# Products with the values in a hybrid attention encoder: the two heads of a pair alternate on TensorE, and the sample's third key tile has 128 rows

## The chip, the cores and the metric

One core of one Trainium2 chip runs the kernel. The metric is the device time of one execution in microseconds (us). One core has TensorE (matrix products), VectorE, ScalarE and GpSimd (elementwise work), SyncE, which mostly issues DMAs, and 16 DMA engines.

## The reference

One step of a two-layer encoder for two request groups that share the weights: a prompt of 256 frames and a sample of 32 frames with 256 cached ones behind it. The model width is 1024, the heads have 64 features, everything is float32.

- Even layer: one input projection feeds 8 heads of chunk-band attention (A) and 8 heads of forgetting attention (B), both with a softmax; then an output projection.
- Odd layer: 16 heads of stick-breaking attention (C): weights from a sum of log-sigmoids over the keys between, no softmax.
- After each: cross-attention into 256 memory tokens (4 heads of 256 features) and a squared-ReLU MLP of width 4096, all with RMS norms and residual adds.

The change concerns the last step of A, B and C, the weighted sum of values:

```python
p = jax.nn.softmax(s, axis=-1).astype(v.dtype)          # A and B
return jnp.einsum('bhqk,bkhd->bqhd', p, v)
...
w = jnp.where(before, jnp.exp(jax.nn.log_sigmoid(z) + tail), 0.0)   # C
return jnp.einsum('bhqk,bkhd->bqhd', w.astype(v.dtype), v)
```

## The kernel before

Activations lie transposed, features on partitions, 288 columns: 256 frames of the prompt and 32 of the sample. Each projection is computed in chunks of 256 output features. A chunk of weights (two tiles "raw") is loaded by SyncE's queue and split into a high part wh (fp32r, ScalarE or VectorE, L143 and L145) and a low part wl (VectorE or GpSimd, L146). A projection is then three products per 128 x 128 block, L160 to L162, into a PSUM tile "g" of 288 columns (256 for the memory's keys and values).

An attention group has four heads, in two pairs p; the two heads of a pair (par = 0, 1) lie in the two halves of 128 partitions. The even layer has groups A0, A1, B0, B1 (`attend_ab`), the odd layer four groups C (`attend_c`). What follows is done per group:

- Scores. In A and B, "ss" holds the sample's scores (L501 and L502: heads of pair 0 into partitions 0 to 63, pair 1 into 64 to 127), and "s" the prompt's scores of one head (L524, L525). In C, "za" and "zb" hold a pair's prompt scores, keys on partitions, and "zs" the sample's (L626, L629 and then L636 to L640).
- Softmax of A and B on VectorE and ScalarE into "pr" (prompt, one head) and "prs" (sample, four heads), then three transposes on TensorE (L530 to L532, L538 to L540) and a copy by ScalarE to "pt" and "pts" in SBUF. In C the weights "w" and "ws" come out with keys on partitions: an ACTIVATE (Exp) and an AFFINE_SELECT on GpSimd that zeroes the upper triangle (L566).
- Products with the values. The stationary operand is a 128 x 64 block of values (one key tile, one head), the moving one the weights. `pv_prompt` is called once per head and issues the product of the first key tile with 256 queries (L469) and of the second with 128 (L470). `pv_sample` issues, for each of four heads, a product with two cached key tiles of 128 rows (L478, L479) and one with the sample's own 32 keys (L480), each with 32 columns. The results stand in the half of the PSUM tile ("po", "za", "pos", "zs") that belongs to the head: partitions 0 to 63 or 64 to 127.
- Evacuation by ScalarE (high part "oh") and VectorE (low part "ol"), which the output projection reads.

The values of the frames are computed by `project_v` into "vT" and transposed into "vt", three key tiles of 256 features; of the third only rows 0 to 31 are written. The cached values "cv" come by DMA.

The program's order on each engine is made by a scheduler when the kernel is built, from the code's order, the pools' buffer counts and its own estimates of time; the two strings ORD_AB and ORD_C give the order in which projections ("q", "p"), groups ("a") and keys of the memory ("K") are handed to it. On an engine, instructions run in that order. "pr" has PRB = 4 buffers, "pt" PTB = 2, "vt" VTB = 2.

## Time and profile before

| | |
|---|---|
| median of 3 runs | 983.2 us (981.46 to 984.86) |
| profiled execution | 983.06 us, span 981.4 us |
| TensorE busy | 971.2 us (99%), 7276 matmul records |
| VectorE busy | 680.5 us (69%) |
| ScalarE busy | 541.6 us (55%) |
| GpSimd busy | 247.7 us (25%) |
| DMA | 160.03 MB, 163 GB/s on average |

The span is the time from the first to the last instruction of the profiled execution; the rest of its 983.06 us lies around it. PE is TensorE's matmuls, PEld its weight loads, DVE VectorE, ACT ScalarE, POOL GpSimd, SP SyncE. A form such as 128*64 behind an operation of PE says how many rows and columns of the array the instruction uses; what follows is the moving operand's size. L12 is line 12 of the kernel.

### The profile page before, as it was taken

Reading aid. Unit: us, or ns where it says so; the run is one execution under the profiler, and the core shown is the slowest. Engines: PE = TensorE matmul, PEld = TensorE weight load, DVE = VectorE, ACT = ScalarE, POOL = GpSimd, SP = SyncE. Lnnn points to the kernel's source line nnn. Section 1 sums busy time; section 2 is a strip of 40 time slices with the busy share of each in tenths; the row PEclk is TensorE's granted clock in tenths of the full one; section 3 lists DMA queues with packets and bytes.
Section 4 is the critical chain, followed back from the end, with each engine's and each line's share of the span. In section 5 each row is a group of like instructions: output and inputs, shape, how many; then the busy total and the mean of one; then the engine's idle time right before and its main releaser. Section 6 shows DMA issues by size and latency. Waiting matters only on the chain.

```text
span 981.4 us, 19371 instructions
## 1 busy us (share of the span) xinstructions
PE 971.2 (99%) x7276; PEld 935.6 (95%) x7276; DVE 680.5 (69%) x1460; ACT 541.6 (55%) x1272; POOL 247.7 (25%) x275
## 2 busy tenths in 40 slices
PE   8999999999999999999999999999999999999998
PEld 8998888899999999999999888889999999999998
DVE  7778778679587767676786555758996766564643
ACT  5667666556456635454656567746554665453531
POOL 4321562222112221122122332323443211111110
PEclk9999999999999999999999999999999999999999
DMA  8654454654545545545565434246444555545552
GB/s 265 198 177 148 146 165 161 213 163 144 172 160 170 169 158 169 168 156 170 170 213 170 144 121 142 97 154 207 145 147 135 169 164 163 166 161 171 168 170 74
DMA packets 50702, 160.03 MB, mean 163 GB/s; under 512 B 6296, under 2 KB 12968, under 8 KB 50352
## 3 DMA queue, kind: packets, MB, share of 16 engines
q1 hardware_dynamic: 46864, 148.69, 47.3%
q0 software_dynamic: 2592, 8.92, 2.4%
q10 hardware_dynamic: 1152, 1.18, 0.4%
q8 instruction: 57, 0.93, 0.4%
q14 instruction: 37, 0.30, 0.1%
HBM read 148.65 MB, written 10.12 MB: 162 GB/s over the span
## 4 chain that ended last, share of the span: by engine, by line
PE 97%; DVE 1%; DMA 1%; ACT 0%; issue 0%; SPq 0%; ACTq 0%; DVEq 0%
PE g L160 28%; PE g L162 27%; PE g L161 27%; PE po L469 1%; PE za L469 1%; PE s L524 1%; PE za L586 1%; DMA raw<-in_w_kv_dram 1%; PE zs L626 0%; PE sx L160 0%; PE za L607 0%; PE sx L162 0%; DMA raw<-in_ab_w_dram 0%; PE pox L162 0%; PE ps_px L698 0%; PE pos L478 0%
## 5 line engine op out<-in xcount | busy, mean ns | idle before, releaser
L145 ACT ACTIVATE wh<-raw 128x512 fp32r<-128x512 f32 (+3 forms) x561 | 279.5, 550 | 231.7 <-PE g L161 120.8
L146 DVE TENSOR_TENSOR wl<-raw,wh 128x512 fp32r<-128x512 f32 (+3 forms) x483 | 306.6, 669 | 111.9 <-ACT wh L145 106.2
L146 POOL TENSOR_TENSOR wl<-raw,wh 128x512 fp32r<-128x512 f32 (+2 forms) x141 | 177.0, 1255 | 540.7 <-ACT wh L145 438.3
L161 PE MATMUL g<-xl,wh 128*128 128x288 f32 (+1 forms) x1032 | 304.0, 297 | 1.5 <-DVE xl L198 1.5
L160 PE MATMUL g<-xh,wh 128*128 128x288 f32 (+1 forms) x1032 | 302.8, 298 | 0.7 <-DVE vT L429 0.4
L162 PE MATMUL g<-xh,wl 128*128 128x288 f32 (+1 forms) x1032 | 302.0, 297 | 0.0
L161 PEld LDWEIGHTS g<-xl,wh 128*128 128x128 f32 (+1 forms) x1032 | 193.6, 188 | 2.6 <-DVE xl L198 1.8
L160 PEld LDWEIGHTS g<-xh,wh 128*128 128x128 f32 (+1 forms) x1032 | 192.6, 188 | 2.4 <-DVE vT L429 0.7
L162 PEld LDWEIGHTS g<-xh,wl 128*128 128x128 f32 (+1 forms) x1032 | 192.9, 188 | 1.1 <-issue 0.2
L161 PE MATMUL g<-hl,wh 128*128 128x288 f32 x512 | 150.3, 295 | 0.0
L160 PE MATMUL g<-hh,wh 128*128 128x288 f32 x512 | 148.9, 295 | 0.0
L162 PE MATMUL g<-hh,wl 128*128 128x288 f32 x512 | 148.5, 294 | 0.0
L161 PEld LDWEIGHTS g<-hl,wh 128*128 128x128 f32 x512 | 96.1, 188 | 0.0
L162 PEld LDWEIGHTS g<-hh,wl 128*128 128x128 f32 x512 | 95.7, 188 | 0.0
L160 PEld LDWEIGHTS g<-hh,wh 128*128 128x128 f32 x512 | 95.3, 187 | 0.0
L161 PE MATMUL g<-ol,wh 128*128 128x288 f32 x256 | 75.7, 298 | 0.0
L160 PE MATMUL g<-oh,wh 128*128 128x288 f32 x256 | 74.6, 299 | 0.6 <-ACT oh L488 0.6
L162 PE MATMUL g<-oh,wl 128*128 128x288 f32 x256 | 74.6, 298 | 0.0
L781 DVE TENSOR_TENSOR h<-h,g 128x288 f32<-128x288 f32 x64 | 28.8, 450 | 29.6 <-PE g L162 29.5
L160 PEld LDWEIGHTS g<-oh,wh 128*128 128x128 f32 x256 | 48.0, 190 | 1.0 <-ACT oh L488 0.8
L162 PEld LDWEIGHTS g<-oh,wl 128*128 128x128 f32 x256 | 48.3, 191 | 0.6 <-issue 0.6
L161 PEld LDWEIGHTS g<-ol,wh 128*128 128x128 f32 x256 | 48.8, 190 | 0.0
(323 smaller groups left out, 1554.8 us busy)
## 6 DMA issues: line engine op xcount, KB each, us to landing
raw<-in_w_up_dram SPq DMA_DIRECT2D x64, 512.0 KB, 3.8
raw<-in_w_down_dram SPq DMA_DIRECT2D x64, 512.0 KB, 3.8
raw<-in_w_kv_dram SPq DMA_DIRECT2D x32, 512.0 KB, 3.9
raw<-in_sb_w_dram SPq DMA_DIRECT2D x24, 512.0 KB, 4.5
raw<-in_ab_w_dram SPq DMA_DIRECT2D x22, 512.0 KB, 4.8
raw<-in_w_q_dram SPq DMA_DIRECT2D x16, 512.0 KB, 4.5
raw<-in_w_o_dram SPq DMA_DIRECT2D x16, 512.0 KB, 4.0
raw<-in_ab_wo_dram SPq DMA_DIRECT2D x8, 512.0 KB, 3.9
```

Source lines behind the costliest of these rows:

```text
L145: act(wh[:, r, :], src, AF.Copy)
L146: e.tensor_tensor(wl[:, r, :], src, wh[:, r, :].bitcast(F32), ALU.subtract)
L160: mm(out, lh, rh, start=first, stop=False)
L161: mm(out, lh, rl, start=False, stop=False)
L162: return mm(out, ll, rh, start=False, stop=last)
L469: mm(dst[:, 0:NP_], vt[:, 0, cols], pt0, start=True, stop=False)
L524: mm(s[:, 0:NP_], q[:, P:NP_], kT[:, p, 0:NP_], start=True, stop=True)
L586: mm(za2, x[:, 0:P], y, start=f_, stop=False, skip_group_check=True)
L781: dve.tensor_tensor(h[:, kt, :], h[:, kt, :], ps[:, 0:T], ALU.add)
```

## The change

`pv_prompt` takes both heads of a pair at once and issues, for each key tile, first head 0 and then head 1. In A and B it is called after the second head's softmax and copy, so "pt" of both heads must be kept (PTB = 3). `pv_sample` goes over key tiles first, then pairs, then heads, and its third product has all 128 rows: the third tile of "vt" is zeroed by a memset before its 32 rows are written, "prs" becomes a tile of 384 columns in the ring of "pr" whose last 96 columns are zeroed, and in C the columns of "ws" that hold the third tile are zeroed. The third transpose of the sample's weights thereby has the full form, and one copy brings all three to SBUF. The branches under SR = 0, which are never taken, are removed.

```diff
-PTB = 2
+PTB = 3
...
         vt = R.ph.tile([P, 3, CW], F32, tag="vt", name="vt", bufs=VTB)
+
+        nc.gpsimd.memset(vt[:, 2, :], 0.0)
...
-    def pv_prompt(po, par, p, vt, pt0, pt1):
-
-        cols = slice(p * P + 64 * par, p * P + 64 * par + 64)
-        dst = po[64 * par:64 * par + 64, :]
-        mm(dst[:, 0:NP_], vt[:, 0, cols], pt0, start=True, stop=False)
-        mm(dst[:, P:NP_], vt[:, 1, cols], pt1, start=False, stop=True)
-
-    def pv_sample(po, cv, vt, pts, pcol):
-        for p in range(2):
+    def pv_prompt(po, p, vt, pts):
+        for kk in range(2):
             for par in range(2):
                 cols = slice(p * P + 64 * par, p * P + 64 * par + 64)
-                dst = po[64 * par:64 * par + 64, p * NS:(p + 1) * NS]
-                q = slice(pcol(p, par), pcol(p, par) + NS)
-                mm(dst, cv[:, 0, cols], pts[0][:, q], start=True, stop=False)
-                mm(dst, cv[:, 1, cols], pts[1][:, q], start=False, stop=False)
-                mm(dst, vt[0:NS, 2, cols], pts[2][0:NS, q], start=False, stop=True)
+                mm(po[64 * par:64 * par + 64, kk * P:NP_], vt[:, kk, cols], pts[par][kk], start=kk == 0, stop=kk == 1)
+
+    def pv_sample(po, cv, vt, pts, pcol):
+        vs = (cv[:, 0, :], cv[:, 1, :], vt[:, 2, :])
+        for kk in range(3):
+            for p in range(2):
+                for par in range(2):
+                    cols = slice(p * P + 64 * par, p * P + 64 * par + 64)
+                    q = slice(pcol(p, par), pcol(p, par) + NS)
+                    mm(po[64 * par:64 * par + 64, p * NS:(p + 1) * NS], vs[kk][:, cols], pts[kk][:, q],
+                       start=kk == 0 and p == 0, stop=kk == 2, skip_group_check=True)
...
-        prs = scr.tile([P, T], F32, tag="f", bufs=FB, name="prs")
-        softmax_rows([s[:, 0:T]], [bsmp], [prs], 1)
+        prs = R.ph.tile([P, 384], F32, tag="pr", name="prs", bufs=PRB)
+        nc.gpsimd.memset(prs[:, T:384], 0.0)
+        softmax_rows([s[:, 0:T]], [bsmp], [prs[:, 0:T]], 1)
         for p in range(2):
-            po = bank(R.o, "po")
+            pts = []
             for par in range(2):
...
-                pv_prompt(po, par, p, vt, pt[:, 0:NP_], pt[:, NP_:NP_ + P])
+                pts.append((pt[:, 0:NP_], pt[:, NP_:NP_ + P]))
+            po = bank(R.o, "po")
+            pv_prompt(po, p, vt, pts)
             put_prompt(oh, ol, kt0 + p, po)
...
-        nc.tensor.transpose(pp[0:NS, 2 * P:3 * P], prs[:, NP_:T], ident)
+        for kk in range(3):
+            nc.tensor.transpose(pp[:, kk * P:(kk + 1) * P], prs[:, kk * P:(kk + 1) * P], ident)
         pt = R.ph.tile([P, 384], F32, tag="pt", bufs=PTB, name="pts")
-        act(pt[:, 0:2 * P], pp[:, 0:2 * P], AF.Copy)
-        act(pt[0:NS, 2 * P:3 * P], pp[0:NS, 2 * P:3 * P], AF.Copy)
+        act(pt, pp[:, 0:3 * P], AF.Copy)
...
-            for par in range(2):
-                pv_prompt(po, par, p, vt, w[:, par * NP_:(par + 1) * NP_], w[:, 512 + par * P:512 + (par + 1) * P])
+            pv_prompt(po, p, vt, [(w[:, par * NP_:(par + 1) * NP_], w[:, 512 + par * P:512 + (par + 1) * P])
+                                  for par in range(2)])
...
         w = R.ph.tile([P, 768], F32, tag="pr", name="ws", bufs=4)
+        nc.gpsimd.memset(w[:, 2 * P:384], 0.0)
```

The order on TensorE changes in three ways. Line numbers of the changed kernel are others: its L473 is L469 and L470 of before, L483 is L478 to L480, L505 and L506 are L501 and L502, L516 and L517 are L524 and L525, L522 to L524 are L530 to L532, L159 to L161 are L160 to L162, L618 and L621 are L626 and L629, and L533 is L538 to L540.

The first place is the sample's products of the third group of the odd layer ("zs" is their PSUM tile, "ws" the weights, "cv" and "vt" the values). Before, with six more rows like these behind them:

```order
L160 MATMUL g<-mh,wh 128x256
L478 MATMUL zs<-ws,cv 64x32
L479 MATMUL zs<-ws,cv 64x32
L480 MATMUL zs<-ws,vt 64x32
L478 MATMUL zs<-ws,cv 64x32
L479 MATMUL zs<-ws,cv 64x32
L480 MATMUL zs<-ws,vt 64x32
```

And of the change:

```order
L159 MATMUL g<-mh,wh 128x256
L160 MATMUL g<-ml,wh 128x256
L483 MATMUL zs<-ws,cv 64x32 x8
L483 MATMUL zs<-ws,vt 64x32 x4
L161 MATMUL g<-mh,wl 128x256
```

The eight products with the cache come first, head by head in alternation, then the four with the sample's own keys.

The second place is the first pair of the odd layer, where the weights "w" of a pair meet the values; "zs<-qz,ck" are the sample's scores. Before:

```order
L626 MATMUL zs<-qz,ck 128x64
L469 MATMUL za<-w,vt 64x256
L626 MATMUL zs<-qz,ck 128x64
L470 MATMUL za<-w,vt 64x128
L469 MATMUL za<-w,vt 64x256
L470 MATMUL za<-w,vt 64x128
L629 MATMUL zs<-qz,kT 32x64
```

And of the change:

```order
L618 MATMUL zs<-qz,ck 128x64
L473 MATMUL za<-w,vt 64x256 x2
L473 MATMUL za<-w,vt 64x128 x2
L618 MATMUL zs<-qz,ck 128x64
L621 MATMUL zs<-qz,kT 32x64
```

The four products of the pair, which stood in two places around a score product, stand together. Five of the odd layer's eight pairs stand so; in three something lies between the 256-column and the 128-column products.

The third place is group B0 of the even layer, with the sample's scores "ss" and the first pair's products "po". Before, the scores stand together:

```order
L162 MATMUL g<-xh,wl 128x288
L501 MATMUL ss<-ck,qs 64x256
L502 MATMUL ss<-kT,qs 64x32
L501 MATMUL ss<-ck,qs 64x256
L502 MATMUL ss<-kT,qs 64x32
L530 MATMUL ps_pt<-ident,pr 128x128
```

And of the change, where the first of the four scores stands some 30 rows higher and the last some 30 rows lower:

```order
L330 MATMUL ps_hn<-sh,bdr 128x288
L506 MATMUL ss<-kT,qs 64x32
L505 MATMUL ss<-ck,qs 64x256
L516 MATMUL s<-kT,qz 128x256
L517 MATMUL s<-kT,qz 128x128
L331 MATMUL ps_hn<-sl,bdr 128x288
L473 MATMUL po<-pt,vt 64x256 x2
L473 MATMUL po<-pt,vt 64x128 x2
```

The second pair of the same group:

```order
L331 MATMUL ps_hn<-sl,bdr 128x288
L473 MATMUL po<-pt,vt 64x256
L516 MATMUL s<-kT,qz 128x256
L517 MATMUL s<-kT,qz 128x128
L516 MATMUL s<-kT,qz 128x256
L517 MATMUL s<-kT,qz 128x128
L159 MATMUL g<-xh,wh 128x288
L160 MATMUL g<-xl,wh 128x288
L473 MATMUL po<-pt,vt 64x256
L473 MATMUL po<-pt,vt 64x128 x2
L533 MATMUL ps_pts<-ident,prs 128x128 x3
```

The first pair's four products stand together; the second pair's first product stands alone, and the other three follow behind scores and projections. In the even layer two of eight pairs are like the first, six like the second.

## Rows read from the trace of the kernel before

**Rows 1.** The page: busy time by engine, and the shares of the chain of work that ended last.

```profile
PE 971.2 (99%) x7276; PEld 935.6 (95%) x7276; DVE 680.5 (69%) x1460; ACT 541.6 (55%) x1272; POOL 247.7 (25%) x275
...
PE 97%; DVE 1%; DMA 1%; ACT 0%; issue 0%; SPq 0%; ACTq 0%; DVEq 0%
```

**Rows 2.** Busy time of each engine by stretch: the stretch, its length, then busy us and number of instructions of each engine, the granted share of TensorE's clock, the DMA engines' share and GB/s.

```profile
20.00:180.00 160.00, 157.08 (x1175) 142.75 (x1174) 120.96 (x343) 101.19 (x280) 53.20 (x56) 1.00 0.51 169
...
545.00:658.80 113.80, 113.48 (x833) 99.55 (x831) 67.27 (x126) 74.10 (x170) 32.14 (x52) 1.00 0.39 128
658.80:662.30 3.50, 3.50 (x15) 3.50 (x16) 1.37 (x4) 0.67 (x2) 0.00 (x0) 0.51 0.89 277
```

**Rows 3.** Groups of matmuls by line and shape: one of the sample's products in the odd layer. Columns: line, engine, operation, out and in, form, shape and count; busy us and mean ns of one; idle time before.

```profile
L479 PE MATMUL zs<-ws,cv 128*64 128x32 f32 x32 | 4.5, 223 | 0.0
```

**Rows 4.** Timeline of TensorE's matmuls around one visit of the sample's products in the odd layer: start us, length us, instruction and count.

```profile
562.14 0.29 PE L160 MATMUL g<-xh,wh 128*128 128x288 f32 x1
562.36 0.30 PE L478 MATMUL zs<-ws,cv 128*64 128x32 f32 x2
562.50 0.28 PE L479 MATMUL zs<-ws,cv 128*64 128x32 f32 x2
562.71 0.30 PE L480 MATMUL zs<-ws,vt 32*64 32x32 f32 x2
562.94 0.30 PE L478 MATMUL zs<-ws,cv 128*64 128x32 f32 x2
...
564.44 0.30 PE L480 MATMUL zs<-ws,vt 32*64 32x32 f32 x2
564.66 0.50 PE L586 MATMUL za<-qh,kh 128*128 128x512 f32 x1
```

**Rows 5.** The same view around the products of one head of the prompt in the even layer.

```profile
108.51 0.29 PE L160 MATMUL g<-xh,wh 128*128 128x288 f32 x1
108.74 0.65 PE L469 MATMUL po<-pt,vt 128*64 128x256 f32 x2
109.22 0.38 PE L470 MATMUL po<-pt,vt 128*64 128x128 f32 x2
109.53 0.33 PE L530 MATMUL ps_pt<-ident,pr 128*128 128x128 f32 x1
```

**Rows 6.** The same view around the products of one pair of the prompt in the odd layer.

```profile
649.06 0.29 PE L161 MATMUL g<-ol,wh 128*128 128x288 f32 x1
649.28 0.65 PE L469 MATMUL za<-w,vt 128*64 128x256 f32 x2
649.86 0.40 PE L162 MATMUL g<-oh,wl 128*128 128x288 f32 x1
650.19 0.32 PE L470 MATMUL za<-w,vt 128*64 128x128 f32 x1
650.20 0.43 PE L469 MATMUL za<-w,vt 128*64 128x256 f32 x1
...
650.68 0.38 PE L470 MATMUL za<-w,vt 128*64 128x128 f32 x2
650.99 0.41 PE L160 MATMUL g<-oh,wh 128*128 128x288 f32 x1
651.23 0.30 PE L161 MATMUL g<-ol,wh 128*128 128x288 f32 x1
```

**Rows 7.** The same view around the sample's products with the memory's values (four heads, one per 32 columns of the array, f32, 256 columns).

```profile
260.23 1.09 PE L736 MATMUL poxs<-cmv,ptxs 128*32 128x256 f32 x16
261.25 0.39 PE L160 MATMUL pox<-ph,mvh 128*128 128x256 f32 x1
```

**Rows 8.** Timeline of TensorE's weight loads at the same place.

```profile
260.23 0.61 PEld L736 LDWEIGHTS poxs<-cmv,ptxs 128*32 128x32 f32 x16
```

**Rows 9.** Timeline of TensorE's matmuls around the sample's scores in the even layer (one pair of heads per half of the columns).

```profile
99.06 0.29 PE L162 MATMUL g<-xh,wl 128*128 128x288 f32 x1
99.28 0.66 PE L501 MATMUL ss<-ck,qs 128*64 128x256 f32 x4
99.76 0.26 PE L502 MATMUL ss<-kT,qs 128*64 128x32 f32 x4
99.95 0.33 PE L530 MATMUL ps_pt<-ident,pr 128*128 128x128 f32 x1
```

**Rows 10.** The same view around a score product of the sample with its own 32 keys in the odd layer.

```profile
546.20 0.30 PE L629 MATMUL zs<-qz,kT 128*32 128x64 f32 x2
546.43 0.43 PE L626 MATMUL zs<-qz,ck 128*128 128x64 f32 x2
```

**Rows 11.** Timeline of all engines from the last score product of the sample in the last group of the odd layer: what makes "ws" of it.

```profile
653.15 0.40 PE L640 MATMUL zs<-sps,mtrir 32*32 32x128 f32 x2
...
653.59 0.38 ACT L642 ACTIVATE ws<-zs 128x256 f32<-128x256 f32 x1 [2.11 <-PE zs L640]
...
653.87 0.25 ACT L644 ACTIVATE ws<-zs 32x128 f32<-32x128 f32 x1
...
654.25 0.30 POOL L566 TENSOR_SCALAR_AFFINE_SELECT ws<-ws 32x128 f32<-32x128 f32 x1 [1.72 <-ACT ws L644]
```

**Rows 12.** Groups of matmuls by line and shape: the third and the second transpose of the sample's weights in the even layer.

```profile
L540 PE MATMUL ps_pts<-ident,prs 128*32 128x128 f32 x4 | 1.1, 273 | 0.0
L539 PE MATMUL ps_pts<-ident,prs 128*128 128x128 f32 x4 | 1.1, 272 | 0.0
```

**Rows 13.** Groups of GpSimd's instructions by line and shape: the low part of a weight split, and a memset.

```profile
L146 POOL TENSOR_TENSOR wl<-raw,wh 128x512 fp32r<-128x512 f32 x84 | 122.0, 1453 | 328.7 <-ACT wh L145 293.0 <-PE g L162 20.9 <-DVE wh L143 7.9
...
L246 POOL MEMSET bmask<- 128x256 f32 x1 | 0.3, 331 | 0.0
```

More of the change, by code (lines that the diff above doesn't have):

```diff
@@ L24 @@
 LASTD = 0
-SR = 0
 SMP = 0
@@ L515, in attend_ab @@
                 s = bank(R.s, "s")
-                if SR:
-                    qh = R.ph.tile([P, NP_], F32R, tag="qh", name="qh", bufs=2)
-                    ql = R.ph.tile([P, NP_], F32R, tag="ql", name="ql", bufs=2)
-                    act(qh, q[:, 0:NP_], AF.Copy)
-                    nc.gpsimd.tensor_tensor(ql, q[:, 0:NP_], qh.bitcast(F32), ALU.subtract)
-                    mm3(s[:, 0:NP_], qh[:, P:NP_], ql[:, P:NP_], kh[:, p, :], kl[:, p, :], True, True)
-                    mm3(s[:, NP_:NP_ + P], qh[:, 0:P], ql[:, 0:P], kh[:, p, 0:P], kl[:, p, 0:P], True, True)
-                else:
-                    mm(s[:, 0:NP_], q[:, P:NP_], kT[:, p, 0:NP_], start=True, stop=True)
-                    mm(s[:, NP_:NP_ + P], q[:, 0:P], kT[:, p, 0:P], start=True, stop=True)
+                mm(s[:, 0:NP_], q[:, P:NP_], kT[:, p, 0:NP_], start=True, stop=True)
+                mm(s[:, NP_:NP_ + P], q[:, 0:P], kT[:, p, 0:P], start=True, stop=True)
                 pr = R.ph.tile([P, 384], F32, tag="pr", name="pr", bufs=PRB)
@@ L534, in attend_ab @@
                 act(pt[:, 0:3 * P], pp[:, 0:3 * P], AF.Copy)
-                pv_prompt(po, par, p, vt, pt[:, 0:NP_], pt[:, NP_:NP_ + P])
+                pts.append((pt[:, 0:NP_], pt[:, NP_:NP_ + P]))
+            po = bank(R.o, "po")
+            pv_prompt(po, p, vt, pts)
             put_prompt(oh, ol, kt0 + p, po)
         pp = bank(ps_t, "ps_pts")
-        nc.tensor.transpose(pp[:, 0:P], prs[:, 0:P], ident)
-        nc.tensor.transpose(pp[:, P:2 * P], prs[:, P:2 * P], ident)
-        nc.tensor.transpose(pp[0:NS, 2 * P:3 * P], prs[:, NP_:T], ident)
+        for kk in range(3):
+            nc.tensor.transpose(pp[:, kk * P:(kk + 1) * P], prs[:, kk * P:(kk + 1) * P], ident)
         pt = R.ph.tile([P, 384], F32, tag="pt", bufs=PTB, name="pts")
-        act(pt[:, 0:2 * P], pp[:, 0:2 * P], AF.Copy)
-        act(pt[0:NS, 2 * P:3 * P], pp[0:NS, 2 * P:3 * P], AF.Copy)
+        act(pt, pp[:, 0:3 * P], AF.Copy)
         po = bank(R.o, "pos")
@@ L808, in forget @@
         u, ua = u2[:, 0, :], u2[:, 1, :]
-        zer = R.ph.tile([8, T], F32, tag="pt", name="zer", bufs=2)
+        zer = R.ph.tile([8, T], F32, tag="pt", name="zer", bufs=PTB)
         nc.gpsimd.memset(zer, 0.0)
```

5 lines of the change are left out of this document (removed).

## Prediction

> **What bounds the kernel now.** I read the page first. TensorE has matmuls in flight for 99% of the span, and the chain that ended last runs through TensorE for 97% of its length [rows 1]: time that leaves TensorE's stream leaves the span, as long as the engines that feed it keep up. Then the stretches: the even layer's attention stage (20 to 180 us) and the odd layer's (545 to 659 us) are where the change sits; VectorE is busy for 121.0 of 160.0 us in the first and for 67.3 of 113.8 us in the second, so both have room [rows 2]. Then, since busy time says little about pipelined matmuls, the timeline of TensorE around the products with the values. What counts there is the time from one start to the next. The projection matmuls follow each other at 0.13 us. I call a stretch in which TensorE works on 64 or 32 columns of its array, between two such matmuls, a visit, and its cost is the distance from the matmul before to the matmul behind, less that 0.13 us.
>
> An f32 product shows as two matmul records, which I call passes (four heads in four groups make 16 products of L479, and x32 records [rows 3]).
>
> **Cost of a visit today.**
> Sample products, odd layer [rows 4]: 562.14 to 564.66, so 2.52 - 0.13 = 2.39 us. Inside, two passes of the same form start 0.06 us apart (a pair of L479 lasts 0.28 us, one pass 0.223 [rows 3]: 0.057 between their starts), but each head's third tile has 32 rows instead of 128, and the pairs on the way into that form and out of it take 0.21 and 0.23 us (562.50 to 562.71 to 562.94), where two passes need 0.12. Coming in takes 0.22 us, going out 0.22 us with the last pass.
> Prompt products, even layer [rows 5]: one head per visit, 108.51 to 109.53, so 1.02 - 0.13 = 0.89 us. A 256-column pass streams about 0.22 us (the first 0.27), a 128-column pass 0.11, going out 0.20.
> Prompt products, odd layer [rows 6]: two visits per pair. From 649.06 to 651.23, less three ordinary steps, is 2.17 - 0.40 = 1.77 us: 0.67 for the first (649.06 to 649.86, less 0.13), 1.10 for the second with the slower step behind it (0.24 instead of 0.13).
>
> **What two column parts do side by side.** In the same rows [rows 6] the second pair half already shows it: a 128-column pass of head 0 starts at 650.19 and a 256-column pass of head 1 at 650.20, and all six passes (1.08 us of streaming if they went one by one) are through in 650.19 to 650.99 with the way out. The memory products show it more strongly: 16 passes of 256 columns on four column parts are started and through in 1.09 us, and the next full matmul starts 1.02 us after the first [rows 7], where 16 x 0.22 = 3.5 us of streaming would stand in a row; their 16 weight loads lie within 0.61 us, beside those matmuls [rows 8]. The score products of the sample have both halves with 256 and with 32 columns, and the whole visit costs 99.06 to 99.95, less 0.13, = 0.76 us [rows 9]. So two halves run at the pace of one.
>
> A rule stands against this. The Trainium skill, "TensorE: Matmul & The Clock Gate", section "Part 3: Packing small matmuls — row/col tiling", says that weight loads overlap with matmuls in flight only where the row groups differ; two column halves share all rows, so by it the halves would load and stream one after the other, and what is left is the form change. What that gives is the first rival below; [rows 8] speak against it, since 16 loads of four column parts with the same rows lie inside 0.61 us of matmuls.
>
> **The change, part by part.**
> Sample products, 8 visits. All twelve products now have one form (128 rows, 64 columns) and alternate between the halves. Six products per half are 12 passes at 0.058 us = 0.67 us to the last start; with 0.22 in, 0.15 out, less 0.13, a visit costs 0.93 us: saves 1.46, times 8 = 11.7 us. Bounds: if the halves don't overlap, 24 passes are 1.36 us and a visit 1.60: saves 6.3 us. If passes could follow as densely as the four 32-column ones of [rows 9], which start within 0.26 - 0.22 = 0.04 us (their weights were loaded ahead), 24 would need 0.34 and a visit 0.58: saves 14.5 us. I take 11.7, the nearest row being the same 32-column pass with a weight load for each, on one half.
> Prompt products, odd layer, 8 pairs. In the program's order five pairs now have all four products in one visit, three are split behind the two 256-column ones. Whole: 0.22 + 0.60 + 0.20 - 0.13 + 0.11 = 1.00 us, which is the second visit of today with nothing ahead of it: saves 0.77 x 5 = 3.9. Split: 0.68 + (0.22 + 0.17 + 0.20 - 0.13 + 0.11 = 0.57) = 1.25: saves 0.52 x 3 = 1.6. Together 5.4 us (by unrounded numbers).
> Prompt products, even layer, 8 pairs. Only two pairs are whole (0.89 against 1.78: saves 0.89 x 2 = 1.8). In six the first head's 256-column product is issued alone, before the second head's softmax is through, and the other three follow in a second visit: 0.67 + 0.88 = 1.55 against 1.78: saves 0.22 x 6 = 1.3. Together 3.1 us.
> What the new order takes back. The four score products of the sample in the even layer stood together in all four groups; now B0 has them in three visits (0.67 + 0.67 + 0.32 against 0.76: +0.9) and B1 in two (+0.7); A1 merges three with a prompt visit and is level: +1.6 us. In the odd layer the 32-column scores of the sample (L629) stand alone six times and at the end of another visit twice, where it was four and four; alone costs about 0.25 more (a way in and a way out, 546.20 to 546.43 is the second [rows 10]): +0.5 us.
> The end of the odd layer. The last group's sample products come right behind its last score product, with nothing between. Today the chain from that product (653.15) over two ACTIVATEs to the select's end at 654.55 takes 1.4 us and is hidden by projection matmuls [rows 11]. Now the first two thirds wait for the first ACTIVATE (till 653.97, some 0.6 us after the last pass), the last third for the select: +0.8 us, less 0.35 for the saved form change: +0.45 us.
> Edits at nothing: the third transpose has 128 columns before and after (273 against 272 ns [rows 12]); one ACTIVATE for two in the copy of pts falls on ScalarE, which waits anyway. The memsets (8 of 128x256, 4 of 128x96, 4 of 128x128) cost GpSimd at most 16 x 0.33 us = 5.3 us [rows 13], beside 247.7 us of work in the span [rows 1]; uncovered, each delays one low part of a weight split (L146) by 0.33 us. The third "pt" buffer and the tile prs in the ring of pr cost no time by themselves.
> Sum: -11.7 - 5.4 - 3.1 + 1.6 + 0.5 + 0.45 = -17.6 us. The profiled execution took 983.06 us, 981.4 of it the span, and the median of the runs is 983.2, the same within their spread. 983.1 - 17.6 = 965.5; as the even layer's new order will make TensorE wait a little more here and there, I say 966 us.
>
> **The rivals.**
> 1. The halves run one after the other. Then the sample saves 6.3, whole pairs 0.25 x 2 and 0.13 x 5, split ones nothing, and the order takes back its 2.5: -5, 978 us. Against it: [rows 6, 7, 8]. 5%.
> 2. The feeders decide in the even layer. Its stage gets 4 x 1.46 + 3.1 - 1.6 = 7.3 us shorter; if splits and softmax chains, whose order on VectorE and ScalarE has changed too, can't follow, that gain turns into waits: -10, 973 us. For it: VectorE 76% and ScalarE 63% busy there; against it: 157.1 of 160 us with TensorE busy [rows 2]. 12%.
> 3. Slower: GpSimd becomes the gate. The memset of a vt buffer waits till the group two before has read it, a memset of prs till a place in the ring of pr is free, and behind them on GpSimd's queue stand low parts of weight splits (1.45 us each [rows 13]), for which the projections wait. Eleven memsets can wait so; from 1.6 us of TensorE's wait at each, 17.6 us in all, the kernel is slower; at 2 us it is 987. Against it: GpSimd is busy for a third of the even layer's stage only (53.2 of 160 us [rows 2]). 3%.
> The clock: for 658.8 to 662.3 us it was granted at 0.51 (1.2 GHz of 2.4), right behind the sparse last visits of the odd layer; 15 matmuls instead of 26 ran in it [rows 2], 1.5 to 1.7 us. It may go, or come once more elsewhere: the likeliest case's range is 961.5 to 970.
>
> **How the numbers follow.** The likeliest case has 80%. Within 0.3% (2.9 us) of before is about what a measurement of this kernel can't tell from no change. Range: 961 (sample at its upper bound, dip gone) to 974, which takes in rival 2 and leaves out rivals 1 and 3 and the tails. Faster 0.94, same 0.03, slower 0.03.
>
> **What would show it.** In the profile after: sample visits of about 0.9 us with starts in pairs; whole pairs of 0.9 to 1.0 us; TensorE's idle time in the even layer's stage not above 5 us; the odd layer's last visit with a wait of some 0.6 us for ScalarE. Wrong it would be if sample visits cost 1.6 us (the halves serial), if projections waited for GpSimd's splits behind a memset, or if the even layer's stage kept its length.

## Result, and the profile after

| | before | after |
|---|---|---|
| median of the runs | 982.33 us (981.43 to 984.86, 4 runs) | 973.25 us (970.67 to 975.1, 4 runs) |
| ratio to before, 95% interval | | 0.9898, 0.9874 to 0.9923 |
| profiled execution | 983.06 us | 970.67 us (the fastest of the four) |
| the sample's first cross-attention score (xs) starts at | 241.52 us | 240.92 us |
| odd layer's stage, first score of its sample to last product with the values | 112.47 us | 102.22 us |
| from there to TensorE's last instruction | 319.29 us | 317.74 us |

Faster by 9.1 us, inside the range, against 17.6 us in the sum. The last three lines are starts of TensorE's instructions read from the two timelines; xs is what the expectations below call the first cross-attention score (the prompt's stand 22.6 us ahead of it in either kernel). The odd layer gave 10.25 us; my terms for it are -5.84 - 5.4 + 0.5 + 0.45 = -10.3. The even layer, which should have given 4 x 1.46 + 3.1 - 1.6 = 7.3 us, gave 0.6. The stretch at half the clock behind the odd layer [rows 2] is missing in this execution: -1.55.

The page after: busy time by engine, and the chain that ended last by engine and by line. [rows 1] had TensorE with 97% of the chain; now DMA and VectorE have 3% each and GpSimd 1%, and two transfers and an addition that belong to the biases of the even layer's B groups (bsmp, b) stand among its lines.

```profile
PE 955.4 (99%) x7276; PEld 922.2 (95%) x7276; DVE 681.5 (70%) x1460; ACT 541.6 (56%) x1268; POOL 249.2 (26%) x291
...
PE 91%; DMA 3%; DVE 3%; issue 2%; POOL 1%; ACT 0%; SPq 0%; DVEq 0%; ACTq 0%; POOLq 0%
PE g L159 27%; PE g L161 27%; PE g L160 26%; DVE wl L145 1%; DMA raw<-in_w_kv_dram 1%; DMA bsmp<-cd 1%; PE za L473 1%; PE za L578 1%; DMA b<-cd 1%; PE zs L618 0%; PE s L516 0%; POOL b L844 0%; PE sx L159 0%; PE po L473 0%; PE za L599 0%
```

The stretches after, columns as in [rows 2]: the even layer's attention, a piece inside it, the odd layer's. In the odd layer TensorE is still almost never idle (busy for 103.46 of 104.40 us). In the even layer it is without work for 5.46 us where it was for 2.92 [rows 2], and a piece of 6.8 us runs at a granted 0.50 (1.2 GHz of 2.4), with 16 matmuls in it.

```profile
20.00:180.00 160.00, 154.54 (x1181) 139.14 (x1180) 120.48 (x343) 100.99 (x275) 53.58 (x60) 0.98 0.52 169
143.90:150.70 6.80, 5.18 (x16) 4.10 (x17) 3.85 (x22) 3.77 (x15) 2.01 (x3) 0.50 0.00 0
544.40:648.80 104.40, 103.46 (x839) 93.63 (x838) 67.76 (x127) 73.66 (x170) 32.56 (x58) 1.00 0.44 141
```

The visits in the odd layer, TensorE's timeline: one of the sample (to be held against [rows 4]) and one whole pair of the prompt (against [rows 6]). The sample: 560.20 to 561.25, less 0.13, = 0.92 us where it was 2.39. The pair: 581.90 to 582.93, less 0.13, = 0.90, with a slower step behind it 1.00, where it was 1.77.

```profile
560.20 0.29 PE L159 MATMUL g<-xh,wh 128*128 128x288 f32 x1
560.43 0.66 PE L483 MATMUL zs<-ws,cv 128*64 128x32 f32 x16
560.91 0.40 PE L483 MATMUL zs<-ws,vt 128*64 128x32 f32 x8
561.25 0.50 PE L578 MATMUL za<-qh,kh 128*128 128x512 f32 x1
...
581.90 0.29 PE L161 MATMUL g<-xh,wl 128*128 128x288 f32 x1
582.13 0.87 PE L473 MATMUL za<-w,vt 128*64 128x256 f32 x8
582.93 0.40 PE L159 MATMUL g<-xh,wh 128*128 128x288 f32 x1
```

The end of the odd layer, same view: the last visit waits 0.62 us for ScalarE, as forecast.

```profile
645.66 0.40 PE L632 MATMUL zs<-sps,mtrir 32*32 32x128 f32 x2
646.68 0.66 PE L483 MATMUL zs<-ws,cv 128*64 128x32 f32 x16 [0.62 <-ACT ws L637]
```

Where the even layer's gain went, TensorE's timeline at the end of group B0 (in brackets: idle time and what ended it):

```profile
134.69 0.70 PE L516 MATMUL s<-kT,qz 128*128 128x256 f32 x2 [0.34 <-DVE mx L457]
...
138.60 0.33 PE L522 MATMUL ps_pt<-ident,pr 128*128 128x128 f32 x1 [0.58 <-ACT pt L526]
...
139.07 1.57 PE L473 MATMUL po<-pt,vt 128*64 128x256 f32 x8
140.58 0.55 PE L533 MATMUL ps_pts<-ident,prs 128*128 128x128 f32 x3
141.77 0.66 PE L483 MATMUL pos<-pts,cv 128*64 128x32 f32 x16 [0.64 <-ACT pts L535]
142.25 0.40 PE L483 MATMUL pos<-pts,vt 128*64 128x32 f32 x8
144.95 1.22 PE L317 MATMUL ps_ms<-mssum,ones 128*128 128x256 f32 x2 [2.29 <-POOL mssum L314]
146.74 0.80 PE L320 MATMUL ps_ms<-ones,mssum 128*128 128x1 f32 x3 [0.56 <-ACT memrs L183]
```

The visit itself (141.77 to 142.65) is as cheap as in the odd layer. Behind it TensorE stands for 2.29 us before ps_ms, the product that adds the memory's sum of squares over the partitions, and 143.9, in that wait, is where the clock falls. GpSimd's timeline at the same time shows why. "sqm" are squares of the memory, "mssum" is their running sum, which ps_ms reads:

```profile
124.46 4.67 POOL L313 TENSOR_TENSOR sqm<-mraw 128x256 f32<-128x256 f32 x6
129.09 0.72 POOL L314 TENSOR_TENSOR mssum<-mssum,sqm 128x256 f32<-128x256 f32 x1
...
132.18 0.74 POOL L314 TENSOR_TENSOR mssum<-mssum,sqm 128x256 f32<-128x256 f32 x1
133.84 0.18 POOL L508 MEMSET prs<- 128x96 f32 x1 [0.91 <-PE ps_pt L524]
133.97 2.34 POOL L314 TENSOR_TENSOR mssum<-mssum,sqm 128x256 f32<-128x256 f32 x3
140.04 1.04 POOL L844 TENSOR_TENSOR b<-b,cq 128x512 f32<-128x512 f32 x1 [3.73 <-DMA b<-cd]
141.04 0.73 POOL L314 TENSOR_TENSOR mssum<-mssum,sqm 128x256 f32<-128x256 f32 x1
141.72 0.64 POOL L845 TENSOR_SCALAR_AFFINE_SELECT b<-b 128x512 f32<-128x512 f32 x1
142.32 1.90 POOL L844 TENSOR_TENSOR b<-b,cq 128x1024 f32<-128x1024 f32 x1
144.17 0.73 POOL L314 TENSOR_TENSOR mssum<-mssum,sqm 128x256 f32<-128x256 f32 x1
```

The bias of group B1 waits 3.73 us for its transfer, and the last two of the seven additions of mssum stand behind it on GpSimd. Three others stand behind the memset of prs, which waits 0.91 us for a transpose. The same view of the kernel before has all seven additions ahead of that bias:

```profile
118.84 4.62 POOL L314 TENSOR_TENSOR sqm<-mraw 128x256 f32<-128x256 f32 x6
123.42 0.72 POOL L315 TENSOR_TENSOR mssum<-mssum,sqm 128x256 f32<-128x256 f32 x1
...
125.80 0.75 POOL L315 TENSOR_TENSOR mssum<-mssum,sqm 128x256 f32<-128x256 f32 x1
...
128.41 3.98 POOL L315 TENSOR_TENSOR mssum<-mssum,sqm 128x256 f32<-128x256 f32 x5
140.97 1.08 POOL L851 TENSOR_TENSOR b<-b,cq 128x512 f32<-128x512 f32 x1 [8.57 <-DMA b<-cd]
```

and there ps_ms ran at 136.7 without a wait:

```profile
136.74 0.60 PE L318 MATMUL ps_ms<-mssum,ones 128*128 128x256 f32 x2
```

So TensorE did not come to ps_ms sooner. It came 5.9 us later than before (142.65 against 136.74), but the sum came 12.5 us later (144.90 against 132.39): the squares shown began 5.6 us later, and the bias got in front of the last two additions. The bound of the loss: 2.5 us more idle time, and 5.18 us of matmuls at half the clock, which at full clock take half, 2.6 us (ps_ms itself took 1.22 us where it had taken 0.60). That is 5.1 of the 6.7 us missing in the even layer. Of the other 1.6 us, visits account for some 0.6. Measured as in the prediction, idle time left out, the even layer's four sample visits went from 9.8 to 3.8 us (6.0 saved, 5.84 forecast), but its prompt visits and the sample's scores together only from 17.2 to 16.5 (0.7 saved, 3.1 - 1.6 = 1.5 forecast); the whole pair at 139.07 alone took 1.51 us where a whole pair of the odd layer takes 0.90. The last 1.0 us these rows don't place.

### The profile page after: what moved, and what is told of

The parts are those of the page before. It is cut to its first block, busy times and chain, and to the rows that moved or that the text cites. A ratio compares the mean times of both kernels' runs of the same rounds, so it can differ in the third digit from the quotient of the medians.

```text
span 969.0 us, 19373 instructions
## 1 busy us (share of the span) xinstructions
PE 955.4 (99%) x7276; PEld 922.2 (95%) x7276; DVE 681.5 (70%) x1460; ACT 541.6 (56%) x1268; POOL 249.2 (26%) x291
## 4 chain that ended last, share of the span: by engine, by line
PE 91%; DMA 3%; DVE 3%; issue 2%; POOL 1%; ACT 0%; SPq 0%; DVEq 0%; ACTq 0%; POOLq 0%
PE g L159 27%; PE g L161 27%; PE g L160 26%; DVE wl L145 1%; DMA raw<-in_w_kv_dram 1%; DMA bsmp<-cd 1%; PE za L473 1%; PE za L578 1%; DMA b<-cd 1%; PE zs L618 0%; PE s L516 0%; POOL b L844 0%; PE sx L159 0%; PE po L473 0%; PE za L599 0%
## 5 line engine op out<-in xcount | busy, mean ns | idle before, releaser
L145 DVE TENSOR_TENSOR wl<-raw,wh 128x512 fp32r<-128x512 f32 (+3 forms) x483 | 315.7, 687 | 113.7 <-ACT wh L144 107.5
L145 POOL TENSOR_TENSOR wl<-raw,wh 128x512 fp32r<-128x512 f32 (+2 forms) x141 | 175.0, 1241 | 530.8 <-ACT wh L144 430.7
L159 PE MATMUL g<-xh,wh 128*128 128x288 f32 (+1 forms) x1032 | 303.1, 298 | 1.1 <-ACT wh L144 0.7
L161 PE MATMUL g<-xh,wl 128*128 128x288 f32 (+1 forms) x1032 | 302.9, 298 | 1.3 <-DVE wl L145 1.2
L160 PE MATMUL g<-xl,wh 128*128 128x288 f32 (+1 forms) x1032 | 303.8, 297 | 0.0
L161 PEld LDWEIGHTS g<-xh,wl 128*128 128x128 f32 (+1 forms) x1032 | 193.0, 188 | 4.0 <-DVE wl L145 2.6
L159 PEld LDWEIGHTS g<-xh,wh 128*128 128x128 f32 (+1 forms) x1032 | 192.5, 188 | 2.7 <-ACT wh L144 0.9
L160 PEld LDWEIGHTS g<-xl,wh 128*128 128x128 f32 (+1 forms) x1032 | 193.4, 188 | 0.9 <-DVE xl L197 0.2
L160 PE MATMUL g<-hl,wh 128*128 128x288 f32 x512 | 150.3, 295 | 0.0
L159 PE MATMUL g<-hh,wh 128*128 128x288 f32 x512 | 148.9, 295 | 0.0
L161 PE MATMUL g<-hh,wl 128*128 128x288 f32 x512 | 148.5, 294 | 0.0
L160 PEld LDWEIGHTS g<-hl,wh 128*128 128x128 f32 x512 | 96.1, 188 | 0.0
L161 PEld LDWEIGHTS g<-hh,wl 128*128 128x128 f32 x512 | 95.7, 188 | 0.0
L159 PEld LDWEIGHTS g<-hh,wh 128*128 128x128 f32 x512 | 95.3, 187 | 0.0
L160 PE MATMUL g<-ol,wh 128*128 128x288 f32 x256 | 75.0, 295 | 0.0
L161 PE MATMUL g<-oh,wl 128*128 128x288 f32 x256 | 74.3, 295 | 0.0
L159 PE MATMUL g<-oh,wh 128*128 128x288 f32 x256 | 73.7, 295 | 0.3 <-ACT oh L492 0.3
L161 PEld LDWEIGHTS g<-oh,wl 128*128 128x128 f32 x256 | 47.9, 188 | 0.4 <-issue 0.4
L160 PEld LDWEIGHTS g<-ol,wh 128*128 128x128 f32 x256 | 48.0, 188 | 0.0
L764 ACT ACTIVATE squ<-tu 128x288 f32<-128x288 f32 x64 | 27.9, 437 | 35.8 <-DVE tu L762 35.7
```

The source lines that it names most:

```text
L145: e.tensor_tensor(wl[:, r, :], src, wh[:, r, :].bitcast(F32), ALU.subtract)
L159: mm(out, lh, rh, start=first, stop=False)
L160: mm(out, lh, rl, start=False, stop=False)
L161: return mm(out, ll, rh, start=False, stop=last)
L764: act(sq, t, AF.Square)
```

## Experiments

Two theories. **A**: the even layer's gain is real and was eaten by the order in which GpSimd and TensorE now meet the memory's sums. **B** (rival 2 of the prediction): the even layer is set by its feeders, and what TensorE saves there turns into waits wherever one looks. In the odd layer, the terms of the sum were tested one by one. The step M is the memory's split and its sum of squares. In what follows "xs" is the start of the sample's first cross-attention score and "odd" the odd layer's stage, both of the profiled execution (before 241.5 and 112.5, after 240.9 and 102.2); the ratio is to the kernel before on the same chip. One xs is a rough figure. The odd layer's part alone has the kernel before's order on every engine up to xs, and its xs is 240.0 against 241.5; the run with 32 rows and that with the odd prompt by head have the changed kernel's order there, and theirs are 246.9 and 242.5 against 240.9. So what the even layer is worth is read from the ratios, and xs says only where to look.

**The additions on VectorE.**

```
-                    nc.gpsimd.tensor_tensor(ssum[:, 0:NP_], ssum[:, 0:NP_], sq[:, 0:NP_], ALU.add)
+                    dve.tensor_tensor(ssum[:, 0:NP_], ssum[:, 0:NP_], sq[:, 0:NP_], ALU.add)
```

> The changed kernel with one edit: in the first layer the sums of squares of the memory (mssum) are added on VectorE instead of GpSimd. Theory A (TensorE stands still behind B0's sample products because the last mssum addition is behind the bias of B1 on GpSimd's queue, and the clock falls after that): the wait of 2.3 us before ps_ms and the low clock from 144 to 151 us go, 5 to 6 us less than the changed kernel, about 967 us median, even layer's stage some 6 us shorter. Rival B (the even layer is held by splits and softmax chains on VectorE and ScalarE, which get 8 more additions): the waits show at other places and the time stays at 973, within 2 us.

Measured: 970.28 us, 0.9858 (0.9835 to 0.988); xs 239.2. The low clock in the even layer is gone and the wait at ps_ms is down to 0.9 us, but new waits at scores and products came; about half of what A claimed in time. Inconclusive between A and B, since VectorE got new work.

**The sample's products head by head**, all with 128 rows.

```
-        for kk in range(3):
-            for p in range(2):
-                for par in range(2):
+        for par in range(2):
+            for p in range(2):
+                for kk in range(3):
```

> The changed kernel with the sample's twelve products issued head by head again (first all of the first half of the columns, then all of the second), but all with 128 rows. Theory A (within one form, each half takes its own instructions in order, and the halves run side by side however they are issued; the gain of the sample comes from the form): a sample visit costs 0.9 us as in the changed kernel, time within 2 us of it. Rival B (the alternation makes the halves overlap): 24 passes in a row, a visit costs 1.6 us, 0.7 x 8 = 5.5 us slower than the changed kernel, about 979.

Measured: 978.04 us, 0.993 (0.9905 to 0.9955); odd 104.3. A visit costs 1.40 us (562.51 to 564.04, less 0.13): between the two forecasts. The timeline of one visit:

```profile
562.51 0.29 PE L159 MATMUL g<-xh,wh 128*128 128x288 f32 x1
562.73 0.42 PE L483 MATMUL zs<-ws,cv 128*64 128x32 f32 x4
562.99 0.28 PE L483 MATMUL zs<-ws,vt 128*64 128x32 f32 x2
563.10 0.42 PE L483 MATMUL zs<-ws,cv 128*64 128x32 f32 x6
...
563.83 0.28 PE L483 MATMUL zs<-ws,vt 128*64 128x32 f32 x2
564.04 0.50 PE L578 MATMUL za<-qh,kh 128*128 128x512 f32 x1
```

The second half's first pass starts at 563.22, when the ninth of the first half's twelve does; only the first half's last four passes run beside the other half, so that 19 steps of about 0.06 us make the 1.16 us from the first start to the last (0.67 when the halves alternate). So the order of issue carries the gain, not the equal form alone.

**The third key tile with 32 rows**, alternating as in the change.

```
-                    mm(po[64 * par:64 * par + 64, p * NS:(p + 1) * NS], vs[kk][:, cols], pts[kk][:, q],
+                    n = P if kk < 2 else NS
+                    mm(po[64 * par:64 * par + 64, p * NS:(p + 1) * NS], vs[kk][0:n, cols], pts[kk][0:n, q],
```

> The changed kernel with the order kept, but the sample's third products with 32 rows instead of 128 (the zeros are written and not read). Theory A (what a change of the form costs is paid once per change, and here one is left per visit): 0.22 in, 7 x 0.058, 0.21 into the 32-row form, about 0.2 in it, 0.15 out, less 0.13: 1.06 us a visit, 0.15 x 8 = 1.2 us slower than the changed kernel at most. Rival B (each 32-row product costs what it did before, with or without company of its kind): four times 0.17 us more, 0.7 us a visit, 5.5 us slower.

Measured: 974.28 us, 0.9909 (0.9889 to 0.9928); xs 246.9 (the profiled execution was the slowest of the four, 977.15), odd 102.7. A visit costs 1.03 us instead of 0.91: with all products of a key tile together there is one change of form in a visit, and the zero fill is worth 0.12 us of the 1.47 saved.

**The even layer's prompt head by head**, the rest as changed (pv_head is the pv_prompt of before under another name; PTB is 2 again).

```
+            po = bank(R.o, "po")
             for par in range(2):
...
-                pts.append((pt[:, 0:NP_], pt[:, NP_:NP_ + P]))
-            po = bank(R.o, "po")
-            pv_prompt(po, p, vt, pts)
+                pv_head(po, par, p, vt, pt[:, 0:NP_], pt[:, NP_:NP_ + P])
```

> The changed kernel with the even layer's prompt products called per head again, as before the change (two pt buffers), everything else as changed. Theory A (the even layer loses its gain to the order on GpSimd, which is the same here: bias of B1 ahead of the last mssum additions; pairing gives 3.1 us and costs 1.6 by split scores): the wait and the low clock stay, 1.5 us slower than the changed kernel at most, about 974. Rival B (it is the pairing in the even layer that makes TensorE wait): the even layer's stage gets 4 us or more shorter than in the changed kernel, 969 or less.

Measured: 972.57 us, 0.9884 (0.9868 to 0.9901); xs 242.8, a wait of 1.7 us at ps_ms and the low clock behind it. The pairing of the prompt is not needed for the loss.

**The odd layer's part alone.** The even layer stands as before in every engine's order (pv_sample_h is the pv_sample of before); beside these lines prs, its transposes, the memset of vt and PTB are as before there.

```
-            pv_prompt(po, p, vt, pts)
+                pv_head(po, par, p, vt, pt[:, 0:NP_], pt[:, NP_:NP_ + P])
...
-        pv_sample(po, cv, vt, [pt[:, 0:P], pt[:, P:2 * P], pt[:, 2 * P:3 * P]], lambda p, par: (2 * p + par) * NS)
+        pv_sample_h(po, cv, vt, [pt[:, 0:P], pt[:, P:2 * P], pt[:, 2 * P:3 * P]], lambda p, par: (2 * p + par) * NS)
```

> The even layer stands as in the kernel before (its prompt and sample products head by head, 32 rows for the sample's third key tile, no fills there); the odd layer has the whole change. Both theories: the even layer up to the first cross-attention score takes 241.5 us as before, the odd layer's stage 102.2 us as in the changed kernel, and the time is 983.2 - 10.25 = about 973. If so, it equals the changed kernel (973.25), and the even layer's half of the change nets nothing. If the even layer's half is worth something that only single runs hide, this kernel is 3 to 7 us slower than the changed one (976 to 980).

Measured: 974.32 us, 0.9898 (0.9883 to 0.9914); xs 240.0, odd 102.3, no wait at ps_ms. The same ratio as the whole change: all that the change does to the even layer nets nothing that these runs can tell.

**The step M one place earlier in the even layer's written order**, in the changed kernel and in the kernel before.

```
-ORD_AB = 'qA0 pA0 F qA1 pA1 aA0 qB0 aA1 qB1 M pB0 pB1 aB0 K2 aB1 K0 K3 K1'.split()
+ORD_AB = 'qA0 pA0 F qA1 pA1 aA0 qB0 aA1 M qB1 pB0 pB1 aB0 K2 aB1 K0 K3 K1'.split()
```

> The changed kernel with one step of the even layer's written order moved: the memory's split and sum of squares (step M) stand ahead of B1's projection instead of behind it, so that GpSimd has the seven additions of mssum ahead of both biases of B1; no work is added or taken away. Theory A (the even layer's gain was eaten by GpSimd's order: B1's bias waits for its transfer and the last mssum additions stand behind it): the wait of 2.3 us at ps_ms goes, the stretch at half the clock behind it (6.8 us, of which half is loss, 3.4) goes too; the even layer up to the first cross-attention score falls from 240.9 to about 235.5 and the time to about 968. Theory B (the even layer is set by its feeders, DVE and ACT, and a wait removed comes back elsewhere): that stage stays at 239 to 241 and the time at 971 to 973.

> The kernel before with the same step M moved ahead of B1's projection, nothing else. Theory A: before has no wait at ps_ms that this could take away, so the time stays at 983 within 1 us. Theory B' (the step's place is worth the same in either kernel, so that it says nothing on the change): it falls by as much as the changed kernel does with it.

Measured: 976.88 us, 0.9929 (0.9913 to 0.9944), xs 249.7; and 988.63 us, 1.006 (1.004 to 1.0079), xs 247.1. Both theories missed. GpSimd's timeline of the first of the two shows the additions, now all ahead of B1's bias, lasting till 118.2; ps_ms has moved ahead with them, and TensorE comes to it 3.4 us too early. The second fence is TensorE's waits from 80 to 200 us (in total, times, longest):

```profile
111.20 0.72 POOL L314 TENSOR_TENSOR mssum<-mssum,sqm 128x256 f32<-128x256 f32 x1
...
113.36 4.87 POOL L314 TENSOR_TENSOR mssum<-mssum,sqm 128x256 f32<-128x256 f32 x6
```

```profile
PE s L516 <- DVE mx L457: 4.3, 2, 3.6
PE ps_ms L317 <- POOL mssum L314: 3.4, 1, 3.4
```

So A in its first form is not the whole story: with the bias out of the way, ps_ms can still come too early. What counts is when the last addition is through against the place that ps_ms has in TensorE's stream. But in all other runs the two go together, which the traces of all 14 kernels show. Where the last two additions stand behind the first instruction of B1's bias (the changed kernel, heads in a row, 32 rows, even prompt by head, odd prompt by head), TensorE waits 1.28 to 2.33 us at ps_ms; where one stands behind it (without fills, below), 2.45 us; where all seven stand ahead of it and TensorE comes to ps_ms at 134 to 137 us (before, the odd layer alone, the sample's order alone, the squares on ScalarE in both kernels), not at all. Left are the additions on VectorE (0.86 us) and the two runs of this section (3.38 and 0.02 us).

**The odd layer's prompt head by head**, the rest as changed.

```
-            pv_prompt(po, p, vt, [(w[:, par * NP_:(par + 1) * NP_], w[:, 512 + par * P:512 + (par + 1) * P])
-                                  for par in range(2)])
+            for par in range(2):
+                pv_head(po, par, p, vt, w[:, par * NP_:(par + 1) * NP_], w[:, 512 + par * P:512 + (par + 1) * P])
```

> The changed kernel with the odd layer's prompt products head by head as before; its sample products and the even layer stay changed. The term of the prediction (eight pairs, 1.77 us down to 1.1 us each): the odd layer's stage grows from 102.2 to 107.6 us and the time to about 978.6. If the two heads' alternation is worth only what the fewer changes of form give, the stage grows by 3 us or less (976).

Measured: 976.31 us, 0.9926 (0.9908 to 0.9944); odd 106.5, so 4.3 us more. The expectation forgot that the scores standing alone (+0.5) and the last visit's wait (+0.45) go with the pairs: 5.4 - 0.95 = 4.45 is what the prediction's terms say. The whole time grew by less, 3.1 us by the medians. The rest of the odd layer's gain, 112.5 - 106.5 = 5.9 us, is the sample's four visits (predicted 5.84).

**The even layer without fills, and with the sample's order alone.** First prs back in its old pool, its transposes and copies as before, 32 rows in the third tile, no memset (PTB stays 3); then also the prompt head by head (PTB 2).

```
-        prs = R.ph.tile([P, 384], F32, tag="pr", name="prs", bufs=PRB)
-        nc.gpsimd.memset(prs[:, T:384], 0.0)
+        prs = scr.tile([P, T], F32, tag="f", bufs=FB, name="prs")
...
-        nc.gpsimd.memset(vt[:, 2, :], 0.0)
+        if R.c:
+            nc.gpsimd.memset(vt[:, 2, :], 0.0)
```

> The changed kernel, but in the even layer nothing is filled on GpSimd: the sample's weights (prs) lie in the pool that they had before, the third key tile is multiplied with its 32 rows, and no memset of vt or prs stands there. The order of products (alternating heads in the even layer's prompt and sample) stays, and the odd layer stays as changed. In its program the step M's sums and ps_ms come back to nearly the place that they have in the kernel before. Theory A (the fills and the pool that prs moved to changed the order in which GpSimd and TensorE meet the memory's sums, and that ate the even layer's gain): no wait above 1.2 us at ps_ms, no stretch of half the clock there, and the even layer up to the first cross-attention score takes 235 to 237 us (before's 241.5 less 4 x 1.3 for the sample and up to 1.5 for the pairs); the time is 967 to 969. Theory B (the layer is set by its feeders, whatever the order): 239 to 241 us there and 972 to 974.

> As the run without fills, and the even layer's prompt products go head by head as before, so that of the change only the order of the sample's twelve products is left in the even layer; its program is that of the kernel before there, but for this order. The odd layer stays as changed. Theory A: the four sample visits save 1.3 us each with nothing reordered: the even layer up to the first cross-attention score takes 236 to 237 us against 240 to 241.5 in the kernel before and in the run with the odd layer alone, and the time is 974.3 - 5.2 = about 969. Theory B: what the visits save is waited for at the next score or transpose, and the time stays at 972 to 974.

Measured: without fills 972.77 us, 0.989 (0.9875 to 0.9906), xs 243.0; sample's order alone 969.43 us, 0.9854 (0.9838 to 0.9869), xs 237.8. The second is what A said: the sample's order alone takes the ratio from 0.9898 (odd layer alone) to 0.9854, 4.3 us where 5.2 were expected. The first is not what A said: the fills are not the only cause. With the pairs back, the same wait stands there, ahead of the same product:

```profile
133.79 0.27 PE L525 MATMUL ps_pt<-ident,pr 128*128 128x128 f32 x1
136.51 1.22 PE L317 MATMUL ps_ms<-mssum,ones 128*128 128x256 f32 x2 [2.45 <-POOL mssum L314]
```

and the clock is low for 10.2 us from 136.0. Pairs in the even layer cost 0.0036 of the time (3.5 us) where the sum had a gain of 3.1; fills with heads apart (the run with the even prompt by head against the sample's order alone) cost 0.003, with intervals that just touch, also with a wait at ps_ms. With either, GpSimd is not through when TensorE comes to ps_ms; both together cost hardly more than one.

**The memory's squares on ScalarE**, in the changed kernel and in the kernel before.

```
-                    nc.gpsimd.tensor_tensor(ssum[:, 0:NP_], m, m, ALU.mult)
+                    act(ssum[:, 0:NP_], m, AF.Square)
...
-                    nc.gpsimd.tensor_tensor(sq[:, 0:NP_], m, m, ALU.mult)
+                    act(sq[:, 0:NP_], m, AF.Square)
```

> The changed kernel with the memory's eight squares (0.78 us each on GpSimd) on ScalarE; the additions stay on GpSimd, and the program puts all of them ahead of both biases of B1, as in the kernel before. Theory A: GpSimd has 6 us less to do ahead of the sums, the wait at ps_ms (2.3 us) and the stretch of half the clock (3.4 us lost) go: even layer up to the first cross-attention score 235 to 237 us, time 967 to 969. Theory B: other waits take its place as with the additions on VectorE (970.3): 239 us there, 970 to 972.

> The kernel before with the memory's eight squares on ScalarE, nothing else: the control for the run that has the same edit in the changed kernel (966.6, or 6.7 below the changed kernel). Theory A (the wait that the edit takes away was made by the change): the kernel before has no wait at ps_ms, so it stays at 983 to 984, within 1.5 us. Theory B' (the squares on GpSimd cost the same in either kernel): it falls by 5 to 7 us, to 977 to 979, and the change itself is worth no more than the 10 us that the comparison shows.

Measured: 966.57 us (964.06 to 967.66), 0.9815 (0.9801 to 0.9829), xs 236.4, odd 102.2; and for the kernel before 983.02 us, 0.9996 (0.9986 to 1.0006), xs 244.1. By its time the edit is worth nothing where the change is not, and with the change it brings back 6.7 us by the medians, more than with the additions on VectorE, the run that made VectorE busier. It beats both kernels. The end of B0 there, by stretch (columns as in [rows 2]):

```profile
130.00:152.00 22.00, 22.00 (x167) 19.07 (x167) 17.75 (x40) 14.10 (x36) 13.72 (x14) 1.00 0.53 183
```

and the same stretch of the changed kernel:

```profile
130.00:152.00 22.00, 17.51 (x118) 13.46 (x117) 10.94 (x47) 10.48 (x35) 11.09 (x14) 0.84 0.40 136
```

167 matmuls at a granted 1.00 against 118 at 0.84. This speaks for A: the lost time hung on GpSimd's share in the memory's sum. It doesn't separate the 6 us that GpSimd is spared from the order that the program takes with them: all additions are again ahead of B1's bias, and ps_ms stands at 135.7 with projections behind it.

## Why the prediction was right, and where its size was off

The time is inside the range because the range took in rival 2, at 973 us; the likeliest case had 961.5 to 970 and was missed. That the loss had just rival 2's size is luck, since its cause was another. Two of the prediction's own signs say so: idle time in the even layer's stage "not above 5 us" was 5.46, and the even layer all but kept its length, which it had named as a sign of being wrong.

- **Sample visits, -1.46 each**: right. 0.91 to 0.92 us measured against 0.93 (the terms as written there add up to 0.91), and 5.9 us for the odd layer's four. The halves go in step: a pass of the second half starts 0.007 us behind one of the first, and each half's passes follow at 0.058 us, as taken from [rows 3].
- **Odd-layer prompts, -5.4**, less 0.95 for lone scores and the last visit: right, 4.3 measured against 4.45; five whole pairs, three split, as counted.
- **Rival 1, halves in a row**: out for the change, as [rows 8] said. Issued head by head, though, the halves do run mostly in a row (1.40 us a visit): what [rows 7, 8] show holds for an order in which the parts take turns, and the prediction had said nothing of another order. The Trainium skill, "TensorE: Matmul & The Clock Gate", section "Part 3: Packing small matmuls — row/col tiling", lets loads overlap only between different row groups; the traces here disagree: with both halves on all 128 rows, the 24 passes of a changed sample visit, each with its own weight load, start within 0.67 us.
- **Even layer, -7.3, "will make TensorE wait a little more"**: this is the step that failed, by its size. I took 0.5 us; it was 6.7. The visits did get cheaper (0.90 to 1.03 for a sample visit, split pairs about 0.67 and 0.88), but in the new order GpSimd had the memory's sum only after TensorE had come to ps_ms, a 2.29 us wait and 6.8 us at half the clock. The prediction named the terms on TensorE's path, priced GpSimd by its memsets and looked at busy shares for the rest ([rows 2]: GpSimd a third busy); that the program's order on GpSimd changes with the edit, it put at nothing. A third busy is an average: from 124 to 145 us GpSimd has seven squares and seven additions with one reader at their end, two of the additions behind a bias whose transfer is late, and in the changed program that reader stands right behind B0's products, with no projection between.
- **Rival 2, the feeders, 973 us**: its time was hit, its reason only in part. The layer isn't bound by VectorE and ScalarE: with the sample's order alone 4.3 us stay, and with ScalarE given eight squares more the total comes near the sum (983.93 - 966.57 = 17.4 us against 17.6). That it comes so near is in part luck: in that run's profiled execution xs is 5.1 us earlier than in the kernel before, where 7.3 were forecast.
- **Rival 3, GpSimd as gate**: right on the engine, wrong on the place. No projection waited for a split behind a memset. What the rival named first, a memset of prs waiting for its place, did happen (0.91 us), but it was additions of mssum that stood behind it. With the prompt head by head the fills cost 0.003 of the time, with intervals that just touch; how much of that is the memset's wait and how much the changed order, no run tells.
- **The clock**: the stretch behind the odd layer went in the profiled run and another came in the even layer. The former is no property of the change: of 14 profiled executions six have it (before, and the additions on VectorE, the heads in a row, the odd layer alone, M earlier in before, the squares on ScalarE), with the odd layer old or new.

## What to carry to other kernels

Price small matmuls on parts of the array by the form changes and by the order of issue: let the parts take turns. A gain on TensorE in a stage with a side chain (here squares and additions on GpSimd with one product at the end) holds only if that chain ends before TensorE comes to its reader. The engine's busy share doesn't tell, and the old trace alone doesn't either: here the chain ended at 132.4 us in the old trace, well ahead of the reader's new time of 142.7, and the wait came because the chain moved too. Look up both places in the new order: what stands ahead of the reader on TensorE, and what now stands ahead of the chain's last step on its own engine, a late transfer above all. Repeat the remedy on the kernel before: an edit that does nothing to the time there and takes 6.7 us off here shows that the loss came with the change.

## What the hardware showed that I had not expected

- Two halves that ran side by side when their passes alternated did so only in part when one was issued after the other: of twelve passes of one half, then twelve of the other, four overlap (1.16 us from first to last start, 0.67 when alternating).
- The wait's own 2.29 us are less than half of its price. The granted clock fell in it, behind a stretch of transposes, column-part products and short waits, and the matmuls of the 6.8 us at 0.50 cost 2.6 us more. The length is not the kernel's own: the run with the odd prompt by head, whose order up to xs is the same, had 10.2 us at 0.50 behind a wait of 2.33 us.
- Two waits of nearly the same length, behind the same products, can end differently. In the run with the squares on ScalarE TensorE stood for 2.07 us ahead of a score product at 105.6 us, and the clock stayed at 1.00. In the run with 32 rows it stood for 2.09 us ahead of the same product, with the same instructions of TensorE before it from 97 us on, and the clock fell to 0.50 for 3.4 us from 106.7. What decided, these rows don't show. The product in the first run and in the second, and then the stretch from 100 to 110 us in the first and in the second (columns as in [rows 2]):

```profile
105.64 0.70 PE L516 MATMUL s<-kT,qz 128*128 128x256 f32 x2 [2.07 <-DVE mx L457]
105.74 0.70 PE L517 MATMUL s<-kT,qz 128*128 128x256 f32 x2 [2.09 <-DVE mx L457]
```

```profile
100.00:110.00 10.00, 7.93 (x55) 6.56 (x54) 10.00 (x26) 6.00 (x16) 4.64 (x4) 1.00 0.32 97
100.00:110.00 10.00, 7.91 (x43) 5.95 (x43) 9.65 (x23) 4.64 (x11) 4.74 (x4) 0.84 0.32 96
```

- Moving the memory's step by one place in the written order cost the kernel before 4.6 us, without a single instruction more.
